# A hybrid decoder layer: fetched value rows added one step later, residual work pinned inside the v loop

## The chip, the cores and the metric

The kernel runs on one core of one Trainium2 chip. The metric is device time in microseconds (us), the median of three runs. Engines: PE (TensorE; PEld is its weight load), DVE (VectorE), ACT (ScalarE), POOL (GpSimd) and SP (SyncE, which only issues DMAs here). Each engine works through its own instructions in order and waits where an instruction needs something that isn't there yet.

## What is computed

A decoder layer for 256 tokens of width 2048: one input projection, a pooling mixer, sparse attention, an output projection, a layer norm, and then PEER, a retrieval over 16384 single-neuron experts, with a second layer norm. The change lies in the last part alone: in PEER's sum over the experts' value rows and in the residual and norm behind it.

```python
def peer_ffn(x, wq, sub_keys, u, v):
    ...                                  # scores, two top-16 lists, expert (t, 8, 16), gate
    act = jax.nn.gelu(jnp.einsum('td,thkd->thk', xc, u_sel), approximate=False)
    return jnp.einsum('thk,thkd->td', (gate * act).astype(x.dtype), v_sel)

h = layer_norm(ALPHA * h + mix, ln1_g[l], ln1_b[l])
ffn = peer_ffn(h, peer_wq[l], peer_subkeys[l], peer_u[l], peer_v[l])
h = layer_norm(ALPHA * h + ffn, ln2_g[l], ln2_b[l])
```

Each token uses 128 experts (8 heads x 16), so `v_sel` has 128 rows of 2048 numbers for each of 256 tokens.

## The kernel before

**Two ways for one sum.** The 256 tokens stand as two halves of 128 (`tt` 0 and 1). For the first 1536 columns the kernel doesn't fetch rows: it multiplies a dense matrix of weights, tokens by experts, with all of v. That matrix is `S` in SBUF, written by the stage before; `step_of(i2)` is its part for 128 experts, and the v loop runs over `i2`, 128 such steps. The last 512 columns (`GV`) are fetched: for each half and each of 128 slots, one indirect DMA on POOL gathers 128 rows of 512 numbers (256 KB) by the indices `e_idx`, 256 gathers in all, and DVE adds each, times its weight in `pd`, into `accg` (L813).

**A step of the v loop** (`i2` from 0 to 123). `weights` splits the step's part of S into a high and a low half, `wt` (ACT copies at L94, DVE subtracts at L95, 128x256). Then come three units of v, `v_d`, of 128x512 (256 KB) each: loaded by SP, split into `hi` (ACT, L94) and `lo` (DVE, L95), with four buffers for each. Each unit gives six matmuls (two halves, three products of high and low parts, L119 to L121) into `vacc` in PSUM, 18 a step. The first units are loaded into `raw` (four buffers, L104); later ones into those parts of S that the loop has used up (L796), by a table worked out ahead (`v_place`, `v_follow`), so that loads run further ahead with each step: five units at first, 22 at step 50, over 40 at the end.

**The gathers.** `spread(i2, 0, GVE)` deals the 256 gathers over steps 0 to 119, 2.1 a step. `add_gathered` issues one and puts its add right behind it in the program. A gather's target is one of three `g` buffers; from step `LEND` = 24 on, when weight units no longer use `raw`, four `raw` buffers join, seven in all. A gather waits until the add that read its buffer last is done.

**The residual.** `residual(c, hf)` is called eight times in steps 32 to 46: it loads two pieces of the first norm's scale and shift (`g1`, in the rows also `g<-ln`, L823) and of the kept activations (`z_dram`, L826) by SP, and multiplies and adds them on POOL (L827, L828) into `pre`. Four loads and four POOL instructions a call.

**The order.** Nothing here is written in its final order. A scheduler sets it, by a planned time for each instruction; `tc.high_priority` moves one forward and `tc.issue_after(x)` keeps one behind x. The residual has no such bound in the kernel before.

**Behind the loop.** The last four steps are not split: `last` holds copies of their parts of S (L854), and 48 matmuls at full precision (L885) close the sums, first for half 0, then for half 1. `finish` (L832) adds ALPHA times the residual to each 512 columns, bn_stats (L857, L889) takes their statistics, and `norm(tt)` scales them: a product on DVE (L870), then for some columns ACT (L874) and POOL (L875), for the others DVE (L877), then the store (L878). The columns 1536 to 2047 of both halves need `accg` complete.

Of the kernel before, what the change touches and what calls it, by code (L numbers as in the profile page):

```python
# [15 lines left out]
ALU = mybir.AluOpType  # L16
AX = mybir.AxisListType

P = 128
T = 256  # L20
NT = T // P
# [36 lines left out]
LEAD = 5  # L58
LAG = 1
KEEP0 = 40  # L60
LEND = 24
GL = 4
GVE = 120
ED = 2
EA = 2
TAIL_POOL = ((0, 1, 2), (0,))
# [5 lines left out]
def layer(ctx, tc, A, out):  # L72
    nc = tc.nc
# [14 lines left out]
        return psB.tile([P, 512], F32, name=name, tag="b")  # L88

    last_split, last_copy, last_load, last_moment = [None], [None], [None], [None]  # L90
    after_unit = [None]

    def split(hi, lo, src, eng=None):
        last_copy[0] = nc.scalar.copy(hi, src).ins  # L94
# [28 lines left out]
    e_idx = small.tile([P, NT, SLOTS], I32, name="e_idx")  # L123
# [3 lines left out]
    z_dram = dram.tile([NT, P, D], F32, name="z_dram")  # L127
# [368 lines left out]
    def step_of(i2, sl=slice(0, T)):  # L496
        return S[:, i2 // 2, sl.start // 2:sl.stop // 2, i2 % 2, :]
# [7 lines left out]
    def paired(a):  # L505
        return a.rearrange("p (t j) -> p t j", j=2)
# [156 lines left out]
    def spread(i, i0, i1):  # L663
        n = i1 - i0
        return gorder[len(gorder) * min(max(i - i0, 0), n) // n:len(gorder) * min(max(i - i0 + 1, 0), n) // n]
# [133 lines left out]
    def v_gather(i2, tt, slot):  # L799
        if i2 >= LEND and count[0] % (GB + RB) >= GB:  # L800
            g = raw_unit()
        else:
            g = gath.tile([P, GV], F32, name="g", bufs=GB)
        count[0] += 1
        nc.gpsimd.indirect_dma_start(out=g, out_offset=None, in_=A["v_g"],  # L805
                                     in_offset=bass.IndirectOffsetOnAxis(ap=e_idx[:, tt, slot:slot + 1], axis=0))
        return g

    def add_gathered(i2):
        with tc.issue_after(last_split[0]):  # L810
            for tt, slot in spread(i2, 0, GVE):
                g = v_gather(i2, tt, slot)
                nc.vector.scalar_tensor_tensor(accg[:, tt], g, pd[:, tt, slot:slot + 1], accg[:, tt],  # L813
                                               op0=ALU.mult, op1=ALU.add)

# [3 lines left out]
    def residual(c, hf):  # L819
        g1 = small.tile([P, 2, T], F32, name="g1", tag="h_gath")  # L820
        sl = slice(c * 512 + hf * T, c * 512 + (hf + 1) * T)
        for i in range(2):
            nc.sync.dma_start(g1[:, i], A["ln1"][i:i + 1, sl].broadcast_to([P, T]))  # L823
        for tt in range(NT):
            o = pre[tt][c][:, hf * T:(hf + 1) * T]
            nc.sync.dma_start(o, z_dram[tt][:, sl])  # L826
            nc.gpsimd.tensor_tensor(o, o, g1[:, 0], op=ALU.mult)  # L827
            nc.gpsimd.tensor_tensor(o, o, g1[:, 1], op=ALU.add)  # L828

    def finish(tt, c, lo, hi, src):  # L830
        o = pre[tt][c][:, lo:hi]
# [4 lines left out]
    for i2 in range(P - GL):  # L836
        wt = weights(i2, tokens if i2 == 0 else [slice(0, T)])
        units = []
        for c in range(NC):
            raw = v_unit(i2, c)  # L840
            units.append(load_unit(A["v_d"][i2 * NC + c], raw))
            if i2:
                for tt in range(NT):
                    product(wt, tt, c, units[c], i2)
        if i2 == 0:
            for tt in range(NT):
                for c in range(NC):
                    product(wt, tt, c, units[c], 0)
        add_gathered(i2)
        if 32 <= i2 < 48 and i2 % 2 == 0:  # L850
            residual((i2 - 32) // 4, (i2 - 32) // 2 % 2)
    last = [big.tile([P, 2, T], F32, name="last", tag="l2"), small.tile([P, 2, T], F32, name="last", tag="h_gath")]
    for j in range(GL):
        nc.scalar.copy(paired(last[j // 2][:, j % 2]), step_of(P - GL + j))  # L854
    for tt in range(NT):
        finish(tt, 3, 512 - GV, 512, accg[:, tt])
        nc.vector.bn_stats(stats[tt][:, 3], pre[tt][3])  # L857
# [96 lines left out]
```

## Time and profile before

| | us |
|---|---|
| median of three runs | 1751.63 (1749.29 to 1753.16) |
| the profiled execution | 1756.99 |
| its span in the trace | 1755.2 |
| first matmul of the v loop that isn't mixed with the stage before | 1176.19 |
| first matmul of the tail (L885) | 1716.38 |
| end of the span | 1755.2 |

The profile is one execution on the chip. Times in its rows are counted from the start of the span. A row of a timeline joins like instructions in a row: start, time from the first's start to the last's end, engine, line, operation, out<-in, count, and in brackets the idle time of the engine before it with what ended it. Matmuls are pipelined, so their shown length (0.40 us) is longer than the distance between two. In a table of stretches each engine has its busy time and its number of instructions, then come the granted clock of TensorE (1.00 is 2.4 GHz), the mean busy share of the 16 DMA engines and the bytes they moved. In the whole execution PE is busy 95% of the span, DVE 83%, ACT and POOL 51%.

### The profile page before, as it was taken

Reading aid. Unit: us, or ns where it says so; the run is one execution under the profiler, and the core shown is the slowest. Engines: PE = TensorE matmul, PEld = TensorE weight load, DVE = VectorE, ACT = ScalarE, POOL = GpSimd, SP = SyncE. Lnnn points to the kernel's source line nnn. Section 1 sums busy time; section 2 is a strip of 40 time slices with the busy share of each in tenths; the row PEclk is TensorE's granted clock in tenths of the full one; section 3 lists DMA queues with packets and bytes.
Section 4 is the critical chain, followed back from the end, with each engine's and each line's share of the span. In section 5 each row is a group of like instructions: output and inputs, shape, how many; then the busy total and the mean of one; then the engine's idle time right before and its main releaser. Section 6 shows DMA issues by size and latency. Waiting matters only on the chain. (4 is left out here: it accounts for less than half of the span.)

```text
span 1755.2 us, 33099 instructions
## 1 busy us (share of the span) xinstructions
PE 1666.4 (95%) x10652; PEld 1484.7 (85%) x10652; DVE 1450.0 (83%) x3515; ACT 897.5 (51%) x1885; POOL 886.7 (51%) x899
## 2 busy tenths in 40 slices
PE   8999999989899999999999889988999999999996
PEld 8999888869888999999999788876687888888883
DVE  6766676679999888889888798877888888889896
ACT  6545565444344555555554358773454555555551
POOL 0000000036775656566565588856747645456562
PEclk9999999989999999999999999998999999999998
DMA  7667657726688999999999841137999999999962
GB/s 219 179 188 192 203 175 261 255 79 214 193 287 268 337 361 321 323 347 336 344 330 329 293 146 55 55 103 255 296 329 333 381 338 332 338 319 328 352 200 89
DMA packets 206014, 451.13 MB, mean 257 GB/s; under 512 B 26928, under 2 KB 31472, under 8 KB 205328
## 3 DMA queue, kind: packets, MB, share of 16 engines
q1 hardware_dynamic: 164816, 297.93, 51.4%
q0 software_dynamic: 41024, 151.09, 24.7%
q8 instruction: 84, 1.38, 0.3%
q14 instruction: 90, 0.74, 0.1%
HBM read 444.59 MB, written 4.26 MB: 256 GB/s over the span
## 5 line engine op out<-in xcount | busy, mean ns | idle before, releaser
L94 ACT CAST hi<-S 128x512 fp32r<-128x512 f32 x677 | 420.4, 622 | 450.5 <-PE vacc L121 223.2
L95 DVE TENSOR_TENSOR lo<-S,hi 128x512 fp32r<-128x512 f32 x672 | 464.5, 701 | 89.6 <-ACT hi L94 81.4
L121 PE MATMUL ups<-hTh,lo 128*128 128x256 f32 x1408 | 392.2, 283 | 11.7 <-DVE lo L95 11.1
L119 PE MATMUL ups<-hTh,hi 128*128 128x256 f32 x1408 | 392.2, 280 | 4.5 <-ACT hi L94 4.2
L120 PE MATMUL ups<-hTl,hi 128*128 128x256 f32 x1408 | 394.0, 281 | 0.0
L659 POOL DMA_INDIRECT g<-u_g,e_idx x256 | 289.2, 1130 | 173.1 <-DVE g L684 119.4
L94 ACT CAST hi<-raw 128x512 fp32r<-128x512 f32 x327 | 202.0, 621 | 245.4 <-PE projT L120 58.9
L95 DVE TENSOR_TENSOR lo<-raw,hi 128x512 fp32r<-128x512 f32 x303 | 216.6, 720 | 111.3 <-ACT hi L94 107.2
L120 PE MATMUL vacc<-lo,wt 128*128 128x512 f32 x744 | 278.4, 401 | 8.6 <-DVE lo L95 8.5
L121 PEld LDWEIGHTS ups<-hTh,lo 128*128 128x128 f32 x1408 | 263.5, 189 | 16.8 <-DVE lo L95 15.6
L121 PE MATMUL vacc<-hi,wt 128*128 128x512 f32 x744 | 276.2, 399 | 0.0
L119 PEld LDWEIGHTS ups<-hTh,hi 128*128 128x128 f32 x1408 | 266.0, 189 | 6.1 <-ACT hi L94 6.1
L120 PEld LDWEIGHTS ups<-hTl,hi 128*128 128x128 f32 x1408 | 265.7, 189 | 0.0
L119 PE MATMUL vacc<-hi,wt 128*128 128x512 f32 x744 | 231.2, 400 | 7.3 <-ACT wt L94 6.9
L805 POOL DMA_INDIRECT g<-v_g,e_idx x139 | 166.3, 1196 | 128.4 <-DVE accg L813 109.0
L684 DVE SCALAR_TENSOR_TENSOR g<-g,h_gath 128x640 f32<-128x640 f32 x256 | 204.9, 820 | 16.6 <-DMA g<-u_g,e_idx 16.1
L805 POOL DMA_INDIRECT raw<-v_g,e_idx x117 | 137.2, 1173 | 84.7 <-DVE accg L813 65.2
L120 PEld LDWEIGHTS vacc<-lo,wt 128*128 128x128 f32 x744 | 141.1, 190 | 45.7 <-DVE lo L95 12.0
L119 PEld LDWEIGHTS vacc<-hi,wt 128*128 128x128 f32 x744 | 141.2, 190 | 42.9 <-ACT wt L94 8.0
L121 PEld LDWEIGHTS vacc<-hi,wt 128*128 128x128 f32 x744 | 140.9, 189 | 34.5 <-issue 0.5
L714 POOL TENSOR_SCALAR bt<-cst,slotT 128x128 f32<-128x128 f32 x192 | 126.3, 675 | 23.3 <-POOL bt L714 16.4
L294 POOL TENSOR_TENSOR bias<-bias,score 128x128 f32<-128x128 f32 (+1 forms) x16 | 11.5, 739 | 233.1 <-DMA bias<-relb 115.8
(243 smaller groups left out, 3074.1 us busy)
## 6 DMA issues: line engine op xcount, KB each, us to landing
S<-v_d SPq DMA_DIRECT2D x361, 256.0 KB, 5.1
S<-u_d SPq DMA_DIRECT2D x328, 256.0 KB, 5.3
raw<-w_t SPq DMA_DIRECT2D x100, 256.0 KB, 2.8
raw<-w_n SPq DMA_DIRECT2D x64, 256.0 KB, 2.8
raw<-w_o SPq DMA_DIRECT2D x64, 256.0 KB, 3.3
raw<-w_q SPq DMA_DIRECT2D x48, 256.0 KB, 3.1
bc<-i_dram SPq DMA_DIRECT2D x32, 256.0 KB, 3.1
raw<-u_d SPq DMA_DIRECT2D x24, 256.0 KB, 5.1
```

What stands on the lines that cost most here:

```text
L94: last_copy[0] = nc.scalar.copy(hi, src).ins
L95: last_split[0] = (eng or nc.vector).tensor_tensor(lo, src, hi.bitcast(F32), op=ALU.subtract).ins
L119: mm(o, l[0], r[0], start=first, stop=False)
L120: mm(o, l[0], r[1], start=False, stop=False)
L121: return mm(o, l[1], r[0], start=False, stop=last).ins
L294: nc.gpsimd.tensor_tensor(bias[:, tt, :n], bias[:, tt, :n], sel[:, tt, :n], op=ALU.add)
L659: nc.gpsimd.indirect_dma_start(out=g, out_offset=None, in_=table, in_offset=bass.IndirectOffsetOnAxis(ap=e_idx[:, tt, slot:slot + 1], axis=0))
L684: nc.vector.scalar_tensor_tensor(g, g, 1.0, h_gath[:, tt], op0=ALU.mult, op1=ALU.mult, accum_out=pd[:, tt, slot:slot + 1])
L714: eng.tensor_scalar(bt[j][:, i], iota, i2T[:, t:t + 1], None, op0=ALU.is_equal)
L805: nc.gpsimd.indirect_dma_start(out=g, out_offset=None, in_=A["v_g"], in_offset=bass.IndirectOffsetOnAxis(ap=e_idx[:, tt, slot:slot + 1], a ...
```

## The change

Four things are altered.

- `add_gathered` keeps the rows it fetched in a list, `fetched`, and adds them in the next step's call; the last call adds what is left.
- The gathers are dealt over steps 10 to 122 (`GV0` = 10, `GVE` = 123) instead of 0 to 119, 2.27 a step, and `LEND` is 10, so all seven buffers are used from the first step with gathers on.
- `residual` stands behind `last_load` (the last weight load issued) and `last_gather` (the last gather issued), for its loads and its POOL instructions alike.
- The four copies into `last` stand behind `last_copy`, the last copy on ACT.

```diff
--- before.py
+++ after.py
@@ -58,9 +58,10 @@
 LEAD = 5
 LAG = 1
 KEEP0 = 40
-LEND = 24
+LEND = 10
 GL = 4
-GVE = 120
+GV0 = 10
+GVE = 123
 ED = 2
 EA = 2
 TAIL_POOL = ((0, 1, 2), (0,))
@@ -88,7 +89,7 @@
         return psB.tile([P, 512], F32, name=name, tag="b")
 
     last_split, last_copy, last_load, last_moment = [None], [None], [None], [None]
-    after_unit = [None]
+    after_unit, last_gather = [None], [None]
 
     def split(hi, lo, src, eng=None):
         last_copy[0] = nc.scalar.copy(hi, src).ins
@@ -802,14 +803,19 @@
         else:
             g = gath.tile([P, GV], F32, name="g", bufs=GB)
         count[0] += 1
-        nc.gpsimd.indirect_dma_start(out=g, out_offset=None, in_=A["v_g"],
-                                     in_offset=bass.IndirectOffsetOnAxis(ap=e_idx[:, tt, slot:slot + 1], axis=0))
+        last_gather[0] = nc.gpsimd.indirect_dma_start(
+            out=g, out_offset=None, in_=A["v_g"],
+            in_offset=bass.IndirectOffsetOnAxis(ap=e_idx[:, tt, slot:slot + 1], axis=0)).ins
         return g
 
+    fetched = []
+
     def add_gathered(i2):
+
         with tc.issue_after(last_split[0]):
-            for tt, slot in spread(i2, 0, GVE):
-                g = v_gather(i2, tt, slot)
+            due = fetched[:]
+            fetched[:] = [(tt, slot, v_gather(i2, tt, slot)) for tt, slot in spread(i2, GV0, GVE)]
+            for tt, slot, g in due:
                 nc.vector.scalar_tensor_tensor(accg[:, tt], g, pd[:, tt, slot:slot + 1], accg[:, tt],
                                                op0=ALU.mult, op1=ALU.add)
 
@@ -819,13 +825,14 @@
     def residual(c, hf):
         g1 = small.tile([P, 2, T], F32, name="g1", tag="h_gath")
         sl = slice(c * 512 + hf * T, c * 512 + (hf + 1) * T)
-        for i in range(2):
-            nc.sync.dma_start(g1[:, i], A["ln1"][i:i + 1, sl].broadcast_to([P, T]))
-        for tt in range(NT):
-            o = pre[tt][c][:, hf * T:(hf + 1) * T]
-            nc.sync.dma_start(o, z_dram[tt][:, sl])
-            nc.gpsimd.tensor_tensor(o, o, g1[:, 0], op=ALU.mult)
-            nc.gpsimd.tensor_tensor(o, o, g1[:, 1], op=ALU.add)
+        with tc.issue_after(last_load[0]), tc.issue_after(last_gather[0]):
+            for i in range(2):
+                nc.sync.dma_start(g1[:, i], A["ln1"][i:i + 1, sl].broadcast_to([P, T]))
+            for tt in range(NT):
+                o = pre[tt][c][:, hf * T:(hf + 1) * T]
+                nc.sync.dma_start(o, z_dram[tt][:, sl])
+                nc.gpsimd.tensor_tensor(o, o, g1[:, 0], op=ALU.mult)
+                nc.gpsimd.tensor_tensor(o, o, g1[:, 1], op=ALU.add)
 
     def finish(tt, c, lo, hi, src):
         o = pre[tt][c][:, lo:hi]
@@ -847,11 +854,14 @@
                 for c in range(NC):
                     product(wt, tt, c, units[c], 0)
         add_gathered(i2)
+        if i2 == P - GL - 1:
+            add_gathered(P)
         if 32 <= i2 < 48 and i2 % 2 == 0:
             residual((i2 - 32) // 4, (i2 - 32) // 2 % 2)
     last = [big.tile([P, 2, T], F32, name="last", tag="l2"), small.tile([P, 2, T], F32, name="last", tag="h_gath")]
-    for j in range(GL):
-        nc.scalar.copy(paired(last[j // 2][:, j % 2]), step_of(P - GL + j))
+    with tc.issue_after(last_copy[0]):
+        for j in range(GL):
+            nc.scalar.copy(paired(last[j // 2][:, j % 2]), step_of(P - GL + j))
     for tt in range(NT):
         finish(tt, 3, 512 - GV, 512, accg[:, tt])
         nc.vector.bn_stats(stats[tt][:, 3], pre[tt][3])
```

What the scheduler makes of it is seen in the order of instructions. The numbers of lines shift by up to ten: L94 is L95, L104 is L105, L796 is L797, L805 is L806, L813 is L819, L826 to L828 are L833 to L835, L832 is L839, L857 is L867, L870 is L880, L889 is L899.

**SP, at the start of the v loop.** Here `raw` and `S` are targets of weight units (`v_d`), `bc` is the stage before, `g_...<-ln` is g1. Before:

```order
L706 DMA bc<-i_dram 128x1024 x28
L104 DMA raw<-v_d 128x512 x2
L823 DMA g_17206<-ln 128x256 x2
L104 DMA raw<-v_d 128x512 x2
L826 DMA pre<-z_dram 128x256 x14
L796 DMA S<-v_d 128x512
L826 DMA pre<-z_dram 128x256 x2
L823 DMA g_17300<-ln 128x256 x2
L104 DMA raw<-v_d 128x512 x5
L796 DMA S<-v_d 128x512 x2
```

and now:

```order
L707 DMA bc<-i_dram 128x1024 x28
L105 DMA raw<-v_d 128x512 x4
L797 DMA S<-v_d 128x512
L105 DMA raw<-v_d 128x512 x5
L797 DMA S<-v_d 128x512 x2
L105 DMA raw<-v_d 128x512 x4
L797 DMA S<-v_d 128x512 x3
L105 DMA raw<-v_d 128x512 x4
L797 DMA S<-v_d 128x512 x4
L105 DMA raw<-v_d 128x512 x2
L797 DMA S<-v_d 128x512 x81
```

The residual's loads stood between units 4 to 8 and are gone from there; the first, for g1, now follow weight unit 113, and the z_dram loads come two at a time with seven weight loads between.

**POOL, behind the stage before.** `bt` is the last of that stage; `g` and `raw` from `v_g` are gathers. Before:

```order
L714 TENSOR_SCALAR bt<-cst,slotT 128x128 x30
L805 DMA g<-v_g,e_idx 128x512 x2
L827 TENSOR_TENSOR pre<-pre,g_17206 128x256
L828 TENSOR_TENSOR pre<-pre,g_17206 128x256
L827 TENSOR_TENSOR pre<-pre,g_17206 128x256
L828 TENSOR_TENSOR pre<-pre,g_17206 128x256
L827 TENSOR_TENSOR pre<-pre,g_17300 128x256 x2
L805 DMA g<-v_g,e_idx 128x512
L828 TENSOR_TENSOR pre<-pre,g_17300 128x256
L805 DMA g<-v_g,e_idx 128x512
L828 TENSOR_TENSOR pre<-pre,g_17300 128x256
L805 DMA g<-v_g,e_idx 128x512 x3
```

and now (the first rows, then those at gather 61):

```order
L715 TENSOR_SCALAR bt<-cst,slotT 128x128 x30
L806 DMA raw<-v_g,e_idx 128x512 x3
L806 DMA g<-v_g,e_idx 128x512 x2
L806 DMA raw<-v_g,e_idx 128x512
L806 DMA g<-v_g,e_idx 128x512
L806 DMA raw<-v_g,e_idx 128x512 x4
L806 DMA g<-v_g,e_idx 128x512 x3
```

```order
L806 DMA raw<-v_g,e_idx 128x512 x2
L834 TENSOR_TENSOR pre<-pre,g_17149 128x256 x2
L835 TENSOR_TENSOR pre<-pre,g_17149 128x256
L806 DMA raw<-v_g,e_idx 128x512
L835 TENSOR_TENSOR pre<-pre,g_17149 128x256
L806 DMA raw<-v_g,e_idx 128x512
L806 DMA g<-v_g,e_idx 128x512 x3
```

The first residual work stood behind gather 5 and now stands behind gather 61; the last stood behind gather 30 and now behind gather 115.

**DVE, at the end of the v loop.** `lo` is the split of a weight unit, `accg` the add of a fetched row, `pre<-pre,vacc` is finish. The last `lo` of the loop is in both pieces. Before:

```order
L95 TENSOR_TENSOR lo<-S,hi 128x512
L813 SCALAR_TENSOR_TENSOR accg<-g,pd,accg 128x512
L95 TENSOR_TENSOR lo<-S,hi 128x512
L813 SCALAR_TENSOR_TENSOR accg<-raw,pd,accg 128x512 x4
L813 SCALAR_TENSOR_TENSOR accg<-g,pd,accg 128x512
L832 SCALAR_TENSOR_TENSOR pre<-pre,vacc 128x512
L813 SCALAR_TENSOR_TENSOR accg<-g,pd,accg 128x512 x2
L889 BN_STATS stats_3593<-pre 128x6
L813 SCALAR_TENSOR_TENSOR accg<-raw,pd,accg 128x512
L832 SCALAR_TENSOR_TENSOR pre<-pre,accg 128x512 x2
L832 SCALAR_TENSOR_TENSOR pre<-pre,vacc 128x512
L857 BN_STATS stats_3593<-pre 128x6
```

and now:

```order
L96 TENSOR_TENSOR lo<-S,hi 128x512
L819 SCALAR_TENSOR_TENSOR accg<-g,pd,accg 128x512
L96 TENSOR_TENSOR lo<-S,hi 128x512
L819 SCALAR_TENSOR_TENSOR accg<-raw,pd,accg 128x512 x4
L819 SCALAR_TENSOR_TENSOR accg<-g,pd,accg 128x512
L839 SCALAR_TENSOR_TENSOR pre<-pre,vacc 128x512
L819 SCALAR_TENSOR_TENSOR accg<-g,pd,accg 128x512 x2
L899 BN_STATS stats_3593<-pre 128x6
L819 SCALAR_TENSOR_TENSOR accg<-raw,pd,accg 128x512 x2
L839 SCALAR_TENSOR_TENSOR pre<-pre,vacc 128x512
L819 SCALAR_TENSOR_TENSOR accg<-raw,pd,accg 128x512 x2
L899 BN_STATS stats_3593<-pre 128x6
```

Behind the last `lo` there were 8 of the 256 adds; now there are 36, 248 and 220 stand ahead of it. The pattern of the piece goes on to the last four rows of adds, which the norm follows:

```order
L819 SCALAR_TENSOR_TENSOR accg<-raw,pd,accg 128x512 x4
L819 SCALAR_TENSOR_TENSOR accg<-g,pd,accg 128x512 x3
L839 SCALAR_TENSOR_TENSOR pre<-pre,accg 128x512
L819 SCALAR_TENSOR_TENSOR accg<-raw,pd,accg 128x512
L867 BN_STATS stats_3593<-pre 128x6
L839 SCALAR_TENSOR_TENSOR pre<-pre,accg 128x512
L435 BN_AGGR mv<-stats_3593 128x2
L867 BN_STATS stats_3594<-pre 128x6
L436 TENSOR_SCALAR mv<-mv 128x1
L880 SCALAR_TENSOR_TENSOR pre<-pre,mv,S 128x512 x4
```

Norm's statistics for half 0 (`stats_3593`) stood among the tail matmuls' finishes; now those of both halves stand behind the last add. In the loop, the first add stands behind the 36th split. From there to the 114th split there are nine adds to twelve splits; from the 115th to the 267th split there are 83 adds, about 1.6 a step; near the end 3 a step, with 4 in two of the steps.

## Rows read from the trace of the kernel before

**Rows 1.** DVE timeline, loop's end: start, us, engine, line, operation, count, [idle].
```profile
1707.77 0.41 DVE L95 TENSOR_TENSOR wt<-S,wt 128x256 fp32r<-128x256 f32 x1
...
1711.97 0.42 DVE L95 TENSOR_TENSOR wt<-S,wt 128x256 fp32r<-128x256 f32 x1
...
1714.43 0.69 DVE L95 TENSOR_TENSOR lo<-S,hi 128x512 fp32r<-128x512 f32 x1
1715.04 2.73 DVE L813 SCALAR_TENSOR_TENSOR accg<-raw,pd,accg 128x512 f32<-128x512 f32 x4
...
1722.62 0.73 DVE L813 SCALAR_TENSOR_TENSOR accg<-raw,pd,accg 128x512 f32<-128x512 f32 x1
```

**Rows 2.** Stretches, PE, the loop's matmuls: busy us (instructions), clock, DMA share, GB/s.
```profile
1176.00:1344.00 168.00, 152.93 (x623) 0.95 0.88 298
1344.00:1716.00 372.00, 372.00 (x1593) 1.00 0.93 322
```

**Rows 3.** PE timeline, start of the loop.
```profile
1176.19 0.50 PE L119 MATMUL vacc<-hi,wt 128*128 128x512 f32 x1 [0.89 <-ACT wt L94]
...
1192.58 1.22 PE L119 MATMUL vacc<-hi,wt 128*128 128x512 f32 x2 [5.87 <-ACT wt L94]
```

**Rows 4.** SP timeline, start of the loop: DMA issues.
```profile
1170.66 7.60 SPq L826 DMA_DIRECT2D pre<-z_dram  x14
...
1185.51 8.36 SPq L104 DMA_DIRECT2D raw<-v_d  x5
```

**Rows 5.** Waits, 1176 to 1344 us: who for whom, us, times, longest.
```profile
DVE accg L813 <- DMA g<-v_g,e_idx: 22.6, 22, 3.1
ACT hi L94 <- DMA raw<-v_d: 13.4, 4, 7.7
```

**Rows 6.** PE timeline, the tail's last matmuls.
```profile
1725.10 13.89 PE L885 MATMUL vacc<-S,last 128*128 128x512 f32 x32
```

**Rows 7.** The page: its span and one row of part 6.
```profile
span 1755.2 us, 33099 instructions
...
S<-v_d SPq DMA_DIRECT2D x361, 256.0 KB, 5.1
```

**Rows 8.** DVE timeline, start of the loop.
```profile
1173.39 0.75 DVE L813 SCALAR_TENSOR_TENSOR accg<-g,pd,accg 128x512 f32<-128x512 f32 x1 [0.23 <-ACT pd L758]
...
1179.24 1.29 DVE L95 TENSOR_TENSOR lo<-raw,hi 128x512 fp32r<-128x512 f32 x2 [2.32 <-ACT hi L94]
```

**Rows 9.** DVE timeline, splits beside POOL's residual work.
```profile
1247.21 2.39 DVE L95 TENSOR_TENSOR lo<-S,hi 128x512 fp32r<-128x512 f32 x2
```

**Rows 10.** Stretches, all engines: PE, PEld, DVE, ACT, POOL, clock, DMA.
```profile
1250.00:1260.00 10.00, 10.00 (x45) 7.89 (x43) 8.15 (x12) 4.99 (x10) 7.51 (x9) 1.00 1.00 323
```

**Rows 11.** Instructions of v_g: their DMAs from issue to landing.
```profile
DMA to landing us min/median/max: 3.4/5.8/9.2
```

**Rows 12.** Stretches, all engines, as rows 10.
```profile
1350.00:1400.00 50.00, 50.00 (x216) 40.22 (x216) 44.90 (x76) 26.44 (x49) 35.08 (x28) 1.00 1.03 374
```

**Rows 13.** POOL timeline, gathers in a row: two runs, first and last.
```profile
742.32 0.96 POOL L659 DMA_INDIRECT g<-u_g,e_idx  x1 [1.81 <-DVE lo L95]
...
756.59 0.95 POOL L659 DMA_INDIRECT g<-u_g,e_idx  x1 [0.30 <-issue]
...
1332.39 0.95 POOL L805 DMA_INDIRECT g<-v_g,e_idx  x1 [0.30 <-DMA g<-v_g,e_idx]
...
1340.24 0.95 POOL L805 DMA_INDIRECT raw<-v_g,e_idx  x1 [0.30 <-issue]
```

**Rows 14.** DVE timeline, the final normalisation.
```profile
1725.07 1.28 DVE L857 BATCH_NORM_STATS2 stats<-pre 128x6 f32<-128x512 f32 x2
...
1740.85 2.73 DVE L870 SCALAR_TENSOR_TENSOR pre<-pre,mv,S 128x512 f32<-128x512 f32 x4
...
1744.45 3.08 DVE L877 SCALAR_TENSOR_TENSOR pre<-pre,mv,S 128x512 f32<-128x512 f32 x3
```

**Rows 15.** POOL timeline, the final normalisation.
```profile
1735.93 3.72 POOL L875 TENSOR_TENSOR pre<-pre,S 128x512 f32<-128x512 f32 x3 [17.35 <-ACT pre L874]
```


## The prediction

> **What bounds the kernel now.** The change touches only the last stage, the v loop: 124 steps, each with three weight units of 128x512 and 18 matmuls, then a tail of 48 matmuls and the final normalisation. I read first the table of stretches for the loop's own matmuls, then the PE timeline at its start, then who waits there, then the end of the loop on DVE, POOL and PE.
>
> The loop has one speed when nothing stops it. At its end the split of a step's weights returns on DVE every 4.20 us (1707.77, 1711.97) [rows 1], so a matmul takes 4.20 / 18 = 0.2333 us. From 1344 to 1716 us 1593 matmuls ran: 1593 x 0.2333 = 371.7 us of 372 [rows 2]. PE is the bound there and nothing can be won. From 1176 to 1344 us 623 ran where 168 / 0.2333 = 720 would fit [rows 2]: 97 are missing, **22.6 us lost**. With the 0.3 us of the second stretch that is 22.9 us, all that the loop can give back. The loss is idle time and what follows it: PE stood 5.87 us before 1192.58 [rows 3], and the granted clock of the stretch is 0.95 against 1.00 later [rows 2]; the pair of matmuls behind that stop took 1.22 us [rows 3].
>
> Two things cause it. SP issued 14 residual loads from 1170.66 on for 7.60 us ahead of the weight loads, whose next five issued from 1185.51 on [rows 4]; ACT waited 13.4 us for raw weights, one wait of 7.7 [rows 5]. And DVE adds a row as soon as its gather is issued, from three buffers: it waited 22.6 us in 22 waits for gathered rows [rows 5], and as DVE works in order the splits that PE needs stood behind them.
>
> After the loop another chain decides. The last split ends at 1715.04 (call this moment **T**: it starts at 1714.43, and the next instruction at 1715.04 [rows 1]). Eight adds are left, the last at 1722.62 [rows 1], all under the tail matmuls, which end at 1725.10 + 13.89 = 1738.99 [rows 6]. So after T PE is the bound for 24 us, then the norm of the second token half for 16.2 us: the span of 1755.2 [rows 7] ends 40.2 us after T.
>
> **The change part by part.** *Residual work to step 32 and later.* The 14 loads and four of the g1 loads leave the front of SP's queue. Weight unit 9 then loads as soon as unit 4's buffer is free (units 4 and 5 were split from 1179.24 on [rows 8]) instead of from 1185.51; weight loads land in 5.1 us at the median [rows 7], so by 1185; unit 9 is needed 45 matmuls (10.5 us) after PE's start at 1176.19 [rows 3], at 1186.7. So the stop of 5.87 us goes, with little to spare. The residual loads now stand between weight loads that run some 15 units ahead, so no weight is late there. The 32 POOL instructions keep their cost and move to steps 36 to 72, beside a PE at full speed. POOL and DVE hold each other up there: two splits took 2.39 us [rows 9] against 1.29 in quiet [rows 8], a loss of 1.1. Four POOL instructions a group thus cost DVE 2 to 3 us, but DVE is four units ahead at most; in the ten microseconds behind those splits, with four more such POOL instructions, PE ran 10.00 of 10.00 [rows 10]. I take 1 us for the eight groups, from 0 to 6.
>
> *Gathers from step 10, seven buffers, adds one step later.* Seven buffers at 256 / 113 = 2.27 rows a step give a row 7 / 2.27 = 3.1 steps, 13 us, from its issue to its add; landing took 3.4 to 9.2, median 5.8 us [rows 11]. The 22.6 us of waits in the loop go. What is late next: DMA. A step asks for 3.5 weight units and 2.27 rows of 256 KB, 1.51 MB in 4.20 us or 360 GB/s; before moved 374 GB/s from 1350 to 1400 with PE at 50.00 of 50.00 [rows 12]. So it is covered, barely. Two adds also leave the front of the loop, where they held up DVE's copies of S (one stood at 1173.39 for 0.75 us [rows 8]); the loop starts some 0.8 us earlier. Left-over stalls: 1 us at the start (0 to 3), 1 for the residual groups, 0.5 near the end, where four adds stand in two of the steps (4 x 0.66 + 3 x 0.61 + 0.34 = 4.8 us of DVE against 4.2). The loop gives 22.9 + 0.8 - 2.5 = **21.2 us**, bounds 15 and 24. T moves to 1693.8.
>
> *What is moved behind the loop.* The order of instructions on DVE is the second half of the story. In steps 39 to 90 it holds about 1.6 adds a step, fewer than the 2.27 gathers due. As DVE works in order, this is binding however fast the chip is. At the last split 220 adds are done and **36 remain, where 8 did**. With seven buffers, gather n + 7 is issued only after add n: at T gather 227 is being issued and 29 are still to come, one after another on POOL.
>
> How far apart are two gathers that wait for nothing? Seven from 1332.39 to 1340.24: 7.85 / 6 = 1.31 us with DVE adding and splitting beside most of them; eleven of u's rows, from 742.32 to 756.59: 1.43, DVE full [rows 13]. The shortest is 0.95 + 0.30 = 1.25. In the tail DVE is some 70% busy (36 adds of 0.66, 12 others of 0.6, in 42 us), so I take 1.32, nearest to the first row; ends 1.25 and 1.43. Gather 256 starts at T + 29 x 1.32 = T + 38.3, lands 3.5 later (DMA is nearly idle, so I take the low end of the landing row [rows 11]) and its add ends at **T + 42.4**. This no longer hides under PE, whose tail ends at T + 24.
>
> Then both token halves are normalised in a row on DVE, since both wait for accg. By the durations of before: two statistics 1.28 [rows 14], one finish and two aggregates about 1.0, twice 2.64 for the four products (2.73 as shown [rows 14]), small ones 1.1: 8.7 us to the first scale. Then four POOL adds, 3.72 for three [rows 15], some 0.8 behind it and pushed by four DVE products (3.08 for three [rows 14]): 6.8. From the last output's readiness to the end, 1755.2 - 1747.53 = 7.7 (the last products end at 1744.45 + 3.08 [rows 14]). Together **23.2** (21 to 24.5).
>
> So the end stands at T + 42.4 + 23.2 = T + 65.6, against T + 40.2: **25.4 us lost** behind the loop. The four copies of `last` to the end are nothing: 0.4 us each on ACT, done before PE reaches the tail 1.3 us after T. Span: 1755.2 - 21.2 + 25.4 = 1759.4, or **+4.2 us**. The profiled execution took 1756.99 in all, 5.4 above the median of the runs shown, 1751.63; I add the difference to the median: **1755.8**.
>
> The bounds: spacing 1.25 takes off 2.0, 1.43 adds 3.2; loop 24 takes off 2.8, 15 adds 6.2; the norm -2.2 to +1.3.
>
> The port. Beside a busy DVE a gather is 0.06 to 0.18 us later than the shortest [rows 13]; a split beside a POOL tensor instruction takes nearly twice as long [rows 9]. The Trainium skill (SBUF — State Buffer, "Who interferes with whom") says that a DVE instruction with two SBUF inputs and a GpSimd instruction that reads SBUF take one shared port in turns, the second waiting out the first; the splits' row agrees, the gathers' rows do so only in small part. By the rule taken fully the time would be that of the third rival below, 1773; by the rows it is 1755.8.
>
> **The rivals.** *The tail's gathers run closer (faster).* Place: POOL behind the loop. If the 0.30 us between two gathers were not part of them, they would follow each 0.95: 29 x 0.37 = 10.7 us less, 1745.1. Below a spacing of 1.06 the change is faster by over 0.2%; at 1.18 it breaks even. For: spans on POOL are rough. Against: among all rows of gathers with nothing to wait for, none follows under 1.25. 0.08.
>
> *The loop keeps half its stalls.* DMA at 360 GB/s, or residual groups that each stop PE for over a microsecond: 10 us kept, 1755.8 + 10 = 1766. For: 360 GB/s from step 10 on is asked while the weights are only five or six units ahead. Against: [rows 10, 12]. 0.11.
>
> *Every gather of the tail waits out an add.* Spacing 1.25 + 0.66 = 1.91: 29 x 0.59 = 17 us more, 1773. Against: 1.43 in [rows 13] with DVE full. 0.03.
>
> *Adds do stand one step behind.* Then about 8 would remain, the end would stay T + 40.2, and the time would be 1751.6 - 21.2 = 1730.4. The order excludes it. 0.01.
>
> **How the numbers follow.** The forecast has 0.77, its own range 1750 to 1761. About 0.2% of this time, 3.5 us, is what a measurement can tell from no change. The forecast lies just beyond it at +4.2, so its chance splits into 0.38 slower, 0.37 within, 0.02 faster. Slower: 0.38 + 0.11 + 0.03 = 0.52; faster: 0.02 + 0.08 + 0.01 = 0.11; within 0.2%: 0.37. The range 1750 to 1765 leaves out the first and the last two rivals (0.12) and some edge of the others.
>
> **What the profile will show.** The stop of 5.87 us and the 22 waits for gathered rows should be gone, and the loop's matmuls at 0.2333 us from about 1175.4 on. The last split should end near 1694, with 36 adds behind it about 1.3 us apart and POOL issuing gathers without a pause; the last add near 1736; PE idle from about 1718. I am wrong if the loop ends later than 1700, or if the last add ends under 38 or over 46 us behind the last split.

## The result, and the profile after

The changed kernel takes **1761.04 us** (median; 1757.07 to 1763.09), the kernel before 1751.71 (1749.29 to 1753.16) in the same comparison: ratio **1.0051**, 95% interval 1.0035 to 1.0067, slower by 6 to 12 us. In a second comparison, with more runs, it was 1762.32 against 1753.68, ratio 1.0057 (1.0039 to 1.0075). The forecast was +4.2 us, 1755.8, with a range of 1750 to 1765. The direction and the mechanism were right, the size was about half.

The first profiled execution of the changed kernel took 1757.07 us with a span of 1755.3, the profiled one of before 1756.99 with 1755.2: the two spans differ by 0.1 us although the medians differ by 9.3. That is a question of its own, and the second pair of traces answers most of it.

The loop, as [rows 2] had it for before (stretch, PE busy with the loop's matmuls, clock, DMA share, GB/s), of the first trace:

```profile
1176.00:1344.00 168.00, 168.00 (x721) 1.00 0.92 320
1344.00:1716.00 372.00, 367.83 (x1537) 1.00 0.90 309
```

In the first stretch 721 matmuls ran where before had 623. That is the full rate. Who waits there for whom (us, times, longest), to be set beside [rows 5]:

```profile
ACT hi L95 <- PE vacc L122: 76.7, 113, 1.2
...
DVE lo L96 <- ACT hi L95: 27.1, 54, 0.7
```

No add waits for a gathered row any more, no split for a raw weight; ACT waits for PE to give buffers back. PE is the bound. The stop of [rows 3] is gone too: the loop begins at 1172.08 and no later pause of PE reaches 0.7 us.

```profile
1172.08 0.50 PE L120 MATMUL vacc<-hi,wt 128*128 128x512 f32 x1 [0.85 <-ACT wt L95]
...
1697.93 13.89 PE L895 MATMUL vacc<-S,last 128*128 128x512 f32 x32
```

The second of these lines answers [rows 6]: the tail's matmuls end at 1711.82, and PE then has nothing to do for 43 us. DVE's timeline says why (as [rows 1]; the first row is the last split):

```profile
1687.35 0.69 DVE L96 TENSOR_TENSOR lo<-S,hi 128x512 fp32r<-128x512 f32 x1
1687.95 2.90 DVE L819 SCALAR_TENSOR_TENSOR accg<-raw,pd,accg 128x512 f32<-128x512 f32 x4
1692.61 0.75 DVE L819 SCALAR_TENSOR_TENSOR accg<-g,pd,accg 128x512 f32<-128x512 f32 x1 [1.76 <-DMA g<-v_g,e_idx]
...
1730.98 0.75 DVE L819 SCALAR_TENSOR_TENSOR accg<-raw,pd,accg 128x512 f32<-128x512 f32 x1
...
1733.62 2.73 DVE L880 SCALAR_TENSOR_TENSOR pre<-pre,mv,S 128x512 f32<-128x512 f32 x4
```

36 adds stand behind the split, each waiting for its row; the last ends at 1731.73, and only then both halves are normalised (the four products of [rows 14] now start at 1733.62) and the span ends 23.6 us later.

From here on a span is cut at two moments. **S** is the start of the second of the two transposes `wTp`, a mark that all kernels share, some 3 us ahead of the loop's first unmixed matmul (3.30 us in both traces of before, 2.64 and 2.63 in those of the changed kernel). **T** is the end of the last split by its own row (1688.04 here, 1715.12 before; the prediction took it 0.08 us earlier). All kernels, from one trace each:

| kernel | S | S to T | adds behind T, last one ends | T to span's end | span |
|---|---|---|---|---|---|
| before, first trace | 1172.9 | 542.2 | 8, T+8.2 | 40.1 | 1755.2 |
| before, second (e1) | 1174.7 | 539.0 | 8, T+8.2 | 40.1 | 1753.8 |
| changed, first trace | 1169.4 | 518.6 | 36, T+43.7 | 67.3 | 1755.3 |
| changed, second (e2) | 1169.0 | 518.6 | 36, T+48.9 | 72.5 | 1760.1 |
| e3, first split pinned | 1168.7 | 549.4 | 3, T+3.4 | 40.6 | 1758.6 |
| e4, residual pin only | 1175.9 | 531.9 | 18, T+24.2 | 51.7 | 1759.4 |
| e5, e3 + early residual | 1168.9 | 537.6 | 3, T+3.3 | 40.6 | 1747.1 |
| e6, early residual only | 1174.5 | 530.8 | 21, T+27.4 | 53.9 | 1759.2 |
| e7, no residual pin | 1171.7 | 534.8 | 20, T+25.1 | 51.6 | 1758.1 |
| e8, e3 + spread residual | 1168.0 | 545.1 | 3, T+3.5 | 40.5 | 1753.6 |
| e9, e3, no arithmetic | 1173.1 | 529.7 | 3, T+2.0 | 40.6 | 1743.3 |
| e10, e8 with even pins | 1168.3 | 529.6 | 3, T+2.0 | 40.1 | 1738.0 |
| e11, e3 with even pins | 1181.9 | 530.1 | 3, T+2.0 | 40.1 | 1752.1 |
| e12, e10, finer residual | 1182.7 | 520.0 | 3, T+2.0 | 40.2 | 1742.9 |

518.6 us from S to T is the loop without a stop. S and the two lengths add up to the span, but for rounding. e11 and e12 come from a comparison in which the kernel before took 1766.85 us, and their S came 6 to 15 us later than elsewhere; the record gives them the same chip as e1 to e4, where the kernel before took 1753.68, and why they differ is open. Of these two only ratios and S to T are compared with the rest. The traced executions of e4 (1761.19 us) and e6 (1761.02) are 7.7 and 5.2 us above the medians of their kernels, so their rows are those of long executions.

### The profile page after: what moved, and what is told of

The parts are those of the page before. It is cut to its first block, busy times and chain, and to the rows that moved or that the text cites. A ratio compares the mean times of both kernels' runs of the same rounds, so it can differ in the third digit from the quotient of the medians.

```text
span 1755.3 us, 33109 instructions
## 1 busy us (share of the span) xinstructions
PE 1658.9 (95%) x10652; PEld 1483.3 (85%) x10652; DVE 1456.7 (83%) x3515; ACT 896.5 (51%) x1885; POOL 874.1 (50%) x899
## 3 DMA queue, kind: packets, MB, share of 16 engines
q1 hardware_dynamic: 164816, 297.93, 51.7%
## 5 line engine op out<-in xcount | busy, mean ns | idle before, releaser
L95 ACT CAST hi<-S 128x512 fp32r<-128x512 f32 x677 | 420.3, 621 | 442.1 <-PE vacc L122 220.2
L660 POOL DMA_INDIRECT g<-u_g,e_idx x256 | 283.7, 1108 | 173.3 <-DVE g L685 122.0
L95 ACT CAST hi<-raw 128x512 fp32r<-128x512 f32 x327 | 201.9, 620 | 231.7 <-PE projT L121 56.8
L806 POOL DMA_INDIRECT raw<-v_g,e_idx x145 | 167.5, 1155 | 158.9 <-DVE accg L819 80.5
L806 POOL DMA_INDIRECT g<-v_g,e_idx x111 | 127.2, 1146 | 87.1 <-DVE accg L819 64.3
```

What stands on the lines that cost most here:

```text
L660: nc.gpsimd.indirect_dma_start(out=g, out_offset=None, in_=table, in_offset=bass.IndirectOffsetOnAxis(ap=e_idx[:, tt, slot:slot + 1], axis=0))
L806: last_gather[0] = nc.gpsimd.indirect_dma_start(out=g, out_offset=None, in_=A["v_g"], in_offset=bass.IndirectOffsetOnAxis(ap=e_idx[:, tt, ...
```

## The experiments

**Second traces of both kernels** (no edit; one chip; e1 is a single execution).

> The kernel before, unchanged, traced a second time. The medians of the two kernels stand 9.3 us apart, their two traces only 0.1 us, so some stage that the change doesn't touch must differ from execution to execution. Theory: in the first trace of before it was not the tail (40.2 us from the last split to the end of the work) and not the start of the loop in v, but something in between or ahead of them; a second trace then shows a span near 1750 with the same 5.87 us stop in the loop and the same 40 us of tail, and one earlier stage 3 to 6 us shorter. Rival: the loop's stalls themselves vary, and the second trace loses clearly less than 22.9 us in the loop (under 19).

> The changed kernel, unchanged, in more rounds and traced a second time. Theory: 1761 us, ratio 1.003 to 1.007; the second trace again runs the loop at 0.233 us a matmul with no stop over 0.7 us, leaves 36 adds behind the last split, and ends 66 to 68 us after it; a time above the first trace's then comes from a stage ahead of the loop. Rival: the gathers of the tail go at another pace from one execution to the next (1.25 us apart in the first trace, up to 1.43), which moves the last add by up to 6 us from T+43.7 towards T+50.

Before: 1755.52 us, span 1753.8. Changed: 1762.32, ratio 1.0057 (1.0039 to 1.0075). Of e1's theory little held: the time was not near 1750, PE's longest stop in the loop was 6.87 us and not 5.87, and the loop lost 20.4 us against 23.6 in the first trace (539.0 and 542.2 less 518.6). So the stalls of before do vary, by 3 us, though less than the rival wanted. Of e2 both sides held something: the loop was the same to 0.1 us, but the last add came at T+48.9, not T+43.7, so the rival was right about what differs between executions of the changed kernel. The gathers of its tail, POOL's timeline, first trace (the bracket is idle time before):

```profile
1704.49 0.95 POOL L806 DMA_INDIRECT raw<-v_g,e_idx  x1 [0.30 <-DMA raw<-v_g,e_idx]
1705.75 0.95 POOL L806 DMA_INDIRECT g<-v_g,e_idx  x1 [0.30 <-DMA raw<-v_g,e_idx]
```

and DVE's adds beside them in the same trace:

```profile
1704.49 0.74 DVE L819 SCALAR_TENSOR_TENSOR accg<-raw,pd,accg 128x512 f32<-128x512 f32 x1
1705.70 0.77 DVE L819 SCALAR_TENSOR_TENSOR accg<-raw,pd,accg 128x512 f32<-128x512 f32 x1 [0.47 <-DMA raw<-v_g,e_idx]
```

Second trace, POOL, then DVE:

```profile
1708.79 1.19 POOL L806 DMA_INDIRECT g<-v_g,e_idx  x1 [0.30 <-issue]
1710.28 1.21 POOL L806 DMA_INDIRECT g<-v_g,e_idx  x1 [0.30 <-issue]
```

```profile
1708.40 0.75 DVE L819 SCALAR_TENSOR_TENSOR accg<-raw,pd,accg 128x512 f32<-128x512 f32 x1
1709.92 0.75 DVE L819 SCALAR_TENSOR_TENSOR accg<-raw,pd,accg 128x512 f32<-128x512 f32 x1 [0.76 <-DMA raw<-v_g,e_idx]
```

In the first trace nearly every gather begins together with an add, within 0.15 us, and takes 0.95: 1.25 us apart. In the second nearly every gather begins while an add is already running, and takes longer by what is left of that add, less 0.13: at 1708.79 the add has 0.36 left and the gather takes 0.24 more; at 1710.28 it has 0.39 left and the gather takes 0.26 more. The fifteen gathers from 1708 to 1730 that met a running add all follow this within 0.02 us. As each add follows its gather's landing, either pattern can keep itself going (this is argued, the traces show only that each lasts): the last twenty gathers stand 1.250 us apart in one trace and 1.440 in the other. 31 gathers start behind T: 31 x 0.19 = 5.9 us, and the tails differ by 5.2.

**The adds kept in the loop.** One edge more on the changed kernel:

```diff
+        with tc.issue_after(step_add.get(i2 - 2)) if i2 - 2 in step_add else nullcontext():
-        wt = weights(i2, tokens if i2 == 0 else [slice(0, T)])
+            wt = weights(i2, tokens if i2 == 0 else [slice(0, T)])
```

> The changed kernel, with one edge more: the first split of a step (VectorE's) has to follow the last add of two steps before. The adds then can't slip behind the loop: 3 stand behind the last split, not 36. Theory (the loop's gain is real, and the 36 adds at 1.25 us alone eat it): the loop still runs at 0.233 us a matmul, the last add comes within 8 us of the last split, and the end is set by TensorE's last products and the second half's norm as in before, 40 us behind the last split: about 1688+40+2 = 1730 us on the trace, 25 to 30 us less than the changed kernel, ratio to before 0.984 to 0.989. Rival: the adds slipped because VectorE or the gathers couldn't keep pace in the loop; then the edge turns the backlog into stops of the splits, the last split comes 20 us or more later, and the time stays above 1745 us.

1760.64 us, ratio 1.0052 (1.0035 to 1.0070). The tail did what the theory said: 3 adds, 40.6 us, 27 to 32 us less than in the changed kernel. The loop gave all of it back: 549.4 us, 30.8 lost. So the rival's outcome, but not its cause. PE's longest stop there (PE timeline):

```profile
1453.12 2.93 PE L122 MATMUL vacc<-hi,wt 128*128 128x512 f32 x6 [3.11 <-DVE wt L96]
```

and all engines in the stretch around it (PE, PEld, DVE, ACT, POOL, clock, DMA):

```profile
1340.00:1470.00 130.00, 114.22 (x442) 86.46 (x441) 106.11 (x155) 50.44 (x98) 85.26 (x79) 0.93 0.89 307
```

PE is idle for 15.8 us of this stretch and the granted clock is 0.93; together this is 27 of the 30.8 us. PE waits for the split of the weights, the very instruction that was pinned; no add in this stretch waited for a gathered row; GpSimd is busy for 85 of 130 us, and its gathers waited 36 us for adds to free their buffers. So GpSimd is not overbooked, and the expectation of e5, which takes it to be, is wrong there. By the order, the edge on one split alone bunches the adds (0 to 5 to every three splits of v) around the very split that PE waits for; e9, e10 and e11 put that to the test.

**One part alone.** e4 is the kernel before with only the residual pin:

```diff
+        with tc.issue_after(last_load[0]), tc.issue_after(last_gather[0]):
             for i in range(2):
                 nc.sync.dma_start(g1[:, i], ...)
```

> The kernel before, with the residual work alone pinned behind its step's last load and last gather; fetches, buffers and adds as before. The order leaves 18 adds behind the last split (8 in before, 36 in the changed kernel). Theory: the one stop of 5.87 us at the residual's place goes, the many short waits for gathers stay (17 of the 22.9 us), and 10 more adds at 1.25 us behind the last split put the norm's start about 12 us later: 1751.7 - 6 + 12 x (the part not hidden beside TensorE's last products; in before the last add came before TensorE was done) = 1745 to 1758. Rival: pinning the residual is what frees the loop, and all 22 us go here already: loop at 0.233 us a matmul with no gather waits, time under 1745.

e7 is the changed kernel without these edges.

> The changed kernel without the pin on the residual work (the residual is free to go early, as in the kernel before); fetch a step ahead, gathers in steps 10 to 122 and seven buffers from step 10 stay. The order leaves 20 adds behind the last split. Theory: the pin is what pushes 16 of the 36 adds behind the loop, and the fetch a step ahead with seven buffers is what frees the loop of its gather waits; the early residual may bring a stop near the loop's start back (up to 5.9 us): 1761.5 - 16 x 1.35 = 1740, plus 0 to 6 us: 1739 to 1747 us. Rival: without the pin the loop's stalls come back in full (over 15 us), time above 1753 us.

e4: 1753.52 us, ratio 1.0010 (0.9992 to 1.0028), inside its theory's 1745 to 1758. e7: 1760.19, ratio 1.0053 (1.0037 to 1.0069). The loop of e4 still loses 13.3 us, that of e7 16.2, that of before 20.4 to 23.6, and that of the changed kernel nothing. Neither part frees the loop alone; e7's theory fell and its rival stands. Which of the later adds, the seven buffers and the later start of the gathers counts inside the second part, no run separates. SP's timeline in e7 shows what the pin is for:

```profile
1169.31 6.82 SPq L832 DMA_DIRECT2D pre<-z_dram  x13
```

and so do the waits of ACT, 1172 to 1270 us:

```profile
ACT hi L95 <- DMA S<-v_d: 19.8, 8, 7.8
ACT hi L95 <- DMA raw<-v_d: 11.5, 5, 6.3
```

The residual's loads again stand ahead of the weights, as in [rows 4]; in the changed kernel ACT has no wait for a weight load in this stretch. The tail follows the count: 18 adds behind T end at T+24.2, 20 at T+25.1, 36 at T+43.7 to 48.9. Both parts add to it: the pin alone 10 adds (8 to 18), the deferral alone 12 (8 to 20), together 28.

**The residual early.** In steps 1 to 8, ahead of the gathers: e5 with e3's edge, e6 without.

```diff
-        if 32 <= i2 < 48 and i2 % 2 == 0:
-            residual((i2 - 32) // 4, (i2 - 32) // 2 % 2)
+        if 1 <= i2 < 9:
+            residual((i2 - 1) // 2, (i2 - 1) % 2)
```

> The kernel of e3_add_pinned with the residual work moved: one block in each of the steps 1 to 8 (ahead of the gathers, which begin in step 10), not one in every second of steps 32 to 46. In e3 the loop stopped by some 30 us, nearly all of it between 1340 and 1460 us, where GpSimd has 32 residual operations of 0.83 to 0.93 us beside 2.27 gathers a step: 2 x 0.9 + 2.27 x 1.4 = 5.0 us of GpSimd's time in a step of 4.2 us. Theory: this overbooking makes the adds late, so with GpSimd free of it the pinned adds keep pace: no stop over 1 us between 1340 and 1460, last split at 1688 to 1694, 3 adds behind it, end 40 us behind: 1728 to 1736 us, ratio 0.985 to 0.991, a version that beats both kernels. Rival: seven buffers, each held over a step, are too few at 2.27 gathers a step wherever the residual stands; then the stops spread over the whole loop and the time stays above 1748 us.

> The changed kernel with the residual work in steps 1 to 8, one block a step, and no edge on the adds. The order leaves 21 adds behind the last split (36 in the changed kernel). Theory: 15 adds fewer at 1.25 to 1.44 us each in the tail are 19 to 22 us; loop still gap-free, last split at 1688, last add at T+25 to T+30, end 23.5 us of norm and 8 us of output later; 1761.5 - 20 = 1738 to 1745 us. Rival: the gathers, not the order, set the last add; GpSimd's queue is as late as before and the last add stays at T+40 or more (above 1752 us).

e5: 1748.58 us, ratio 0.9986 (0.9975 to 0.9998). e6: 1755.78, ratio 1.0027 (1.0013 to 1.0041). Both expectations were too low by over 10 us, for one reason: the loop lost 19.0 and 12.2 us, most of it at its start (13.6 and 12.3 before 1270 us), where SP's loads for the residual stand among those of the weights and ACT waits 26.3 and 29.2 us for weight units. e6's tail was as the theory said (21 adds, T+27.4). e5's loop had no stop over 1 us from 1340 to 1460, as expected; its time is the one that its rival named, its stops are not spread as that rival wanted.

**Spread residual.** e8 is e3 with a residual block in every eighth step of 24 to 80; e10 is e8 with the edge on all splits of a step:

```diff
+            with tc.issue_after(step_add.get(i2 - 2)) if i2 - 2 in step_add else nullcontext():
-            units.append(load_unit(A["v_d"][i2 * NC + c], raw))
+                units.append(load_unit(A["v_d"][i2 * NC + c], raw))
```

e9 is e3 with the residual's GpSimd operations cut to two columns, which leaves most of the residual unscaled: it is a probe, not a version of the kernel.

> The kernel of e3_add_pinned with one residual block in every eighth step of 24 to 80, not in every second of 32 to 46. Of GpSimd's time a block of four operations takes 3.6 us, so 0.45 us a step beside 2.27 x 1.25 to 1.45 = 2.8 to 3.3 us of gathers, under the step's 4.2 us; and the residual's loads stay out of the loop's first 100 us, where e5, e6 and e7 lost 12 to 19 us waiting for transfers. Theory (residual work costs the loop twice: by its loads where it is early, by GpSimd's time where it is dense): both kinds of stop go, the loop loses under 6 us, last split at 1689 to 1695, 3 adds behind it, end 40.6 us behind: 1731 to 1738 us, ratio 0.987 to 0.992. Rival: a pinned add stops VectorE whenever one gather is late, whatever the residual does; stops of 1 to 3 us spread over 1300 to 1600 us, 15 us or more in all, time over 1744 us.

> The kernel of e3_add_pinned with the residual's 32 GpSimd operations cut from 256 columns to 2 (the residual is then left unscaled but for two columns of each block); its loads and its place in steps 32 to 46 stay. Theory (GpSimd's time is overbooked there): the 27 us that the residual's operations take go from GpSimd's queue, the gathers keep pace, and of e3's 30 us of stops in 1340 to 1460 at most 8 stay: 1732 to 1742 us. Rival A: the residual's loads, behind the weights' loads in one queue, delay the gathers' buffers and weights there: stops as in e3, 1755 us or more. Rival B: seven buffers held over a step are too few at this pace, with the same outcome.

> The kernel of e8_spread_pinned with the edge on every split of a step rather than on its first alone, so that the adds stand more evenly between the splits (2 or 3 a step, where e8's order has 0 to 5). Theory: an even order lets fewer adds bunch up behind a late gather; within 4 us of e8, on the lower side. Rival: more splits tied to adds pass every late gather on to TensorE, 4 us or more above e8.

e8: 1756.32 us, 1.0028 (1.0015 to 1.0041), 26.5 us lost in the loop in stops of up to 2.6 us: its theory fell. Its rival's outcome came, but not by the rival's cause, as the loop's adds waited 3.4 us in all for gathered rows. e9: 1744.25, 0.9957 (0.9941 to 0.9973), 11.1 lost in the loop, 7.7 of it from 1340 to 1470 where its theory allowed 8; the time is 2 us above the theory's range and far from the rivals'. **e10: 1742.61, 0.9954 (0.9940 to 0.9968)**, 11.0 lost, 13.7 us below e8 where I expected at most 4. So of e3's 30.8 us 19 to 20 go either way: by taking the arithmetic out under the uneven order (e9), or by dealing the adds evenly with the arithmetic in place (e10, and e11 below with the residual where e3 has it). Neither cause alone explains the stops; they come where both meet. What the arithmetic does is seen on DVE, which it slows: the splits of 1340 to 1470 by line and form (busy us, mean ns), in e3:

```profile
L96 DVE TENSOR_TENSOR lo<-S,hi 128x512 fp32r<-128x512 f32 x76 | 56.5, 773 | 23.9 <-ACT hi L95 23.6
```

and in e9:

```profile
L96 DVE TENSOR_TENSOR lo<-S,hi 128x512 fp32r<-128x512 f32 x87 | 57.7, 689 | 21.7 <-ACT hi L95 20.1 <-DMA pre<-z_dram 1.2
```

A split took 0.773 us on the mean with the residual's arithmetic in the stretch and 0.689 without it. Slow splits alone don't stop PE, though; in the changed kernel, whose loop is whole, they take 0.782 us there:

```profile
L96 DVE TENSOR_TENSOR lo<-S,hi 128x512 fp32r<-128x512 f32 x94 | 72.2, 782 | 12.2 <-ACT hi L95 10.9 <-DMA S<-v_d 0.7 <-DMA g<-ln 0.2
```

**Even pins with either residual.** e11 is e3 with e10's edge; e12 is e10 with each block cut in two (one token half), one in every fifth step of 24 to 99.

> The kernel of e3_add_pinned (residual in every second of steps 32 to 46) with the edge on every split of a step, so that 2 or 3 adds stand in each step and not 0 to 5. It tells apart what e10 gained over e8: Theory (the even order is what counts, the residual's place counts less): of e3's 30 us of stops most go, T some 15 us earlier than e3's 1718, time 1742 to 1750 us. Rival (GpSimd is overbooked in steps 32 to 46, so an even order changes nothing there): 1755 us or more.

> The kernel of e10_spread_loads_pinned with the residual blocks cut in two (two GpSimd operations for one half of the tokens) and one such half in every fifth step of 24 to 99. Theory (e10's 11 us of stops follow its blocks of 3.6 us, each of which delays the gathers behind it): half as long blocks let the gathers pass, stops 3 to 7 us, 1736 to 1741 us, ratio 0.991 to 0.994. Rival: e10's stops come from the gathers and the seven buffers alone; then no change, 1740 to 1745 us.

e11: 1752.34 us, ratio 0.9920 (0.9899 to 0.9940). The time is above its theory's 1742 to 1750, in a comparison in which the kernel before took 13 us more as well. S to T is 530.1, 19.3 less than e3's, with the residual in the same place: the even order alone is worth that here. **e12: 1743.92 us against 1766.85, ratio 0.9867 (0.9846 to 0.9887)**, 8.4 us below e11 in the same comparison. Better than its theory, which left 3 to 7 us of stops; the loop is whole (PE, the loop's matmuls):

```profile
1340.00:1470.00 130.00, 130.00 (x557) 1.00 1.02 364
1186.00:1700.00 514.00, 513.85 (x2197) 1.00 0.95 334
```

It keeps the changed kernel's loop (520.0 against 518.6) and the tail of before (40.2): what the change could have been, with the adds held evenly in their steps and the residual's GpSimd work in small pieces far apart. Whether the smaller pieces or the wider spacing counts, no run separates.

## Why the prediction came out as it did

*The loop gives back 21.2 us, bounds 15 and 24.* Measured 23.6 and 20.4. Right, with its parts: the stop, the 22 waits and the slower start of [rows 3] and [rows 5] are gone. The left-over stalls that I allowed for (2.5 us) did not come; the earlier start of the loop (0.8 us) measured 0.7. The runs add that the two parts need each other (e4, e7).

*36 adds remain; POOL is the bound; the last add ends at T+42.4.* The count and the bound were right. **This is the step that was mis-sized**: T+43.7 in the first trace and T+48.9 in the second, the latter beyond the 46 us at which I said I would be wrong. 31 gathers were to come behind T, not 29 (2 x 1.32 = 2.6 us), and landing with the add took 4.7 us, not 4.1. The spacing was 1.26 on the mean in the first trace, which took 2.0 us off, and 1.43 in the second, which put 3.3 on. I took one value between the two ends of [rows 13]; in the two traces the spacing stood at the one end (nearly every step 1.25) or had the other as its mean (steps of 1.25 to 1.73).

*The norm, 23.2 us.* Measured 23.6 in both traces.

*What I left out: the stage ahead of the loop.* S came 3.5 us earlier in the first pair and 5.7 in the second. No instruction ahead of S is altered, and I had put this stage at nothing (my 0.8 us lie behind S); the last section shows most of it as another rate of matmuls, of open cause.

So for the second pair, e1 and e2: S -5.7, loop -20.4, behind T +32.4, together +6.3, the difference of the spans. For the first pair -3.5 - 23.6 + 27.2 = +0.1: an execution of the changed kernel with its shorter tail beside one of before with its longer loop. That is why the first two traces agree. The comparison of medians gives 8.6 to 9.3. The last 2 to 3 us are not located: both traces of before come from executions above its median (1756.99 against 1751.7, 1755.52 against 1753.7), and what the typical ones do better no trace shows.

*How near it was.* The forecast's own range was 1750 to 1761, and the median of 1761.04 lies at its upper edge. The tail cost 1.8 us more than forecast in the first pair and 7.0 in the second, and the early S, which I had not foreseen, took 3.5 and 5.7 us off again. By an estimate from these numbers the time without it would be 1764.5 to 1766.7, at the end of the stated range or beyond it: that part was luck.

*The rivals.* Tail gathers under 1.25 us apart: no, 1.25 is the shortest seen. The loop keeps half its stalls: no. Every gather waits out an add, 1.91 us apart: in kind this is what the second trace does, in size not, since a gather waits only for part of what is left of the add, 0.48 us at most in that tail (the gather at 1690.06 took 1.43). Adds do stand one step behind: no, 36 stayed behind the loop. The Trainium skill (SBUF — State Buffer, "Who interferes with whom") says that the port pair which the two engines share is an exclusive lock, and that a DVE instruction with two SBUF inputs contends with a GpSimd instruction that reads SBUF; the gathers of e2 agree, prolonged by 0.24 and 0.26 us beside such adds in the rows above. The same section tells of a probe in which a `tensor_tensor` did not stall a DMA of GpSimd's, and infers that such an operation leaves the writing of descriptors alone. Here this differs: the splits are `tensor_tensor` operations with two SBUF inputs, and they hold a gather up as the adds do (e2, POOL, then DVE; 0.47 us of the split are left, and the gather takes 0.34 more than 0.95):

```profile
1641.34 1.29 POOL L806 DMA_INDIRECT g<-v_g,e_idx  x1 [1.31 <-DVE accg L819]
```

```profile
1641.12 0.69 DVE L96 TENSOR_TENSOR lo<-S,hi 128x512 fp32r<-128x512 f32 x1
```

In the two traces of the changed kernel 208 gathers began over 0.06 us into a split with at least 0.2 us of it left, and 190 of them were prolonged by that rest less 0.13 us, to within 0.025 us.

## What to carry to other kernels

Taking a wait out of a loop is worth something only if the work that waited stays in the loop: look in the order at what stands behind the loop's last instruction, and price it one by one. Where an engine works in order, an edge that holds the work in its step must keep it evenly between the instructions that the bound engine waits for; on one of them alone the loop lost 30.8 us here, on all of them 11.5 with the same rest of the kernel. With the one edge and without GpSimd's arithmetic beside it 11.1 us were lost, so such work belongs in small pieces far apart, as in e12. And one trace of each kernel can hide a difference of 9 us: cut both spans at the same moments and compare the pieces, from two executions.

## What was not expected of the hardware

A gather (an indirect DMA of 128 rows issued by GpSimd) that starts while a DVE add or split with two SBUF inputs runs is prolonged by the rest of that instruction less 0.13 us. One that starts with an add mostly isn't: over all fourteen traces 114 of the 121 gathers of v's rows that began in the first 0.06 us of an add took the usual 0.95 us. With a split it was 76 of 159, and what decides between the two is open. That a gather reads its row numbers from SBUF at that moment would fit, and was not tested.

The 256-column matmuls of the stage ahead run at one of two rates, by kernel. From 600 to 940 us (PE busy, matmuls), kernel before:

```profile
600.00:940.00 340.00, 340.00 (x2889) 1.00 0.96 339
```

and the changed kernel:

```profile
600.00:940.00 340.00, 340.00 (x2917) 1.00 0.97 343
```

From one matmul's start to the next it is 117.8 ns on the mean against 116.7, at the same granted clock and with the same order of instructions there on every engine. Before, e1, e4, e6 and e9 have the first, the changed kernel, e2, e3, e5, e7, e8 and e10 the second (e11 and e12, which stop in this stretch, 116.7 and 117.3 between the stops). From its first matmul to its last the stage takes 530.1 and 529.6 us in the traces of before, 525.8 and 526.0 in those of the changed kernel. All these kernels differ in the last stage alone and fall on either side; the cause is open.
